# A layer's modulation vector summed by TensorE instead of VectorE, ScalarE and GpSimd

## The chip, the cores and the metric

The kernel runs on one core of one Trainium2 chip. The metric is the device time of one execution in microseconds; lower is better.

## The reference, cut to what matters

Two blocks run over a sequence of 256 tokens of width 1024. The first block has two layers, and each layer scales, shifts and gates by a vector `mod` of six parts that depends on the conditioning `c` alone:

```python
c_act = jax.nn.silu(c)                                  # (1, 1024)
for l in range(2):
    mod = c_act @ w_mod[l] + b_mod[l]                   # w_mod[l]: 1024 x 6144
    shift1, scale1, gate1, shift2, scale2, gate2 = jnp.split(mod[:, None, :], 6, axis=-1)
    h = rms_norm(x, norm1) * (1.0 + scale1) + shift1
    proj = h @ w_in[l]                                  # q, k, u, v and gates
    mix = concat(pool_mixer(u), nsa_mixer(q, kv, gates)) @ w_out[l]
    x = x + gate1 * mix
    h2 = rms_norm(x, norm2) * (1.0 + scale2) + shift2
    x = x + gate2 * (jnp.square(jax.nn.relu(h2 @ w_ff1[l])) @ w_ff2[l])
```

Then a second block follows (a state space branch, an attention branch and a feed forward). The change touches the modulation of the first layer only: parts 0 to 4 of `mod` (shift1, scale1, gate1, shift2, scale2).

## The kernel before, in words

**Products.** Weights come from HBM in pages of 128 partitions by 1024 f32 (512 KB) into the tile `wst`, which has five buffers. ScalarE rounds a page to `wh` (L140), VectorE takes the rest as `wl` (L141), and each product of the model is three TensorE matmuls in a one-pass format (fp32r): high by low, low by high, high by high. All page loads go through one queue (SP), in the order of the program; a load waits until the last reader of the buffer five pages back is done.

**The first two parts of the vector** (shift1 and scale1 of layer 0) are needed before anything else. `start()` walks over four blocks `c` of 256 columns of both parts. `first_mod(c)` loads four pages; VectorE multiplies one half of each page by `c_act` of that row and sums it (L612, L615), ScalarE multiplies the other half and GpSimd sums it (L613, L616, L617). What is left is a sum over partitions, done by eight matmuls against a matrix of ones in `first_norm` (`tr<-cst,acc`), which then transposes 256 columns of the normalized input and makes `hh` and `hl`. Between the blocks run the products for q and k with that block (L89, `acc<-wh,hl` and the like).

**The next three parts** (gate1, shift2, scale2: the list `MODS["mix", 0]`) are summed page by page by `mod_part` while q, k, u, v, the attention and the output product run. Of eight pages of a part five are taken by VectorE (L548) and three by ScalarE and GpSimd (L550, L551), into a tile `macc`; a sum over partitions by matmuls with ones follows (`tr<-cst,macc`, `mal`, `mah`). The parts are generators: `W.load`, which fetches a weight page, advances them by `W.rate` steps, 0 at first and `r0b` = 2 from step 14 of the layer on. The other parts (lists `ff` and `mix` of the next layer) use the same function later.

**PSUM.** Four banks `acc`, two `st`, one `tr`, one `pv`. `pv` holds the transposes in `first_norm`, later the attention's sums over values (`attn_c`), later the transposes of `to_fm`.

**Order.** Each engine runs its instructions in a fixed order that a list scheduler wrote ahead of time: program order is the priority, but an instruction that its model holds ready may go ahead of an earlier one that is not.

Of the kernel before, what the change touches and what calls it, by code (L numbers as in the profile page):

```python
# [24 lines left out]
ALPHA = 2.0 ** 0.25  # L25

SZ = 1024
TU = dict(nst=5, tabc=2, nw=9, nt2=22, raw=1, krest=2, qrest=4, pool2=1, c2=3, c3=1, c4=1, ln=3, uv='uv', pre=[1], nv=5, nv1=0, nv0=0, u0=19.5, du=0.7, ub=2, uc=4, c0=32.5, dc=0.1, w0=36, dw=0.5, comp=22, pool=27, dpool=2, cmpa=32, cmpb=34, dcmp=2, e1=1, e0=1, pta=2, ahead=3, modp=3, rf=0.95, r0=0, r0b=2, r1=0.8, r1b=1.2, rs=14, raw_=4, qrest_=6, u0_=19.5, du_=1.0, comp_=22, pool_=26, cmpa_=31, cmpb_=35, nv_=0, nv0_=0, w0_=32, dw_=0.8, order2='v0 qk0 qk1 qk2 v1 B C x0 x1 z0 x2 z1 x3 z2 z3 g2 g3 pa g0 g1 ps', dts=8, dcd=30, par0=10, par1=40, d0=50, dd=2, db=3, dc2=5, ss0=73, ds=4.2, scb=5, sx=3, sr=6, sg=3.5, sy=3.5, sn=8, sf=300, mf0=5, modp1=99, rf1=0.5, pool2_=3, c3_=2, c4_=3, nv1_=2, dpool_=2, dcmp_=1, dc_=0.4, cap=4, ub_=2.5, c0_=32.5, pta_=4)
NST, NW = TU['nst'], TU['nw']
NT2, NT4, NS5 = TU['nt2'], 5, 20  # L30

# [30 lines left out]
def tile_two_blocks(ctx: ExitStack, tc: tile.TileContext, I, out, stop=None, dbg=None):  # L62
# [452 lines left out]
    V.reciprocal(cact, cact)  # L515
    V.tensor_tensor(cact, cact, csrc, op=OP.mult)

    parc = [small.tile([128, NPS], FT, name=f"parc{l}", bufs=1) for l in range(DEPTH)]
    par = {}

# [5 lines left out]
    def PS(l, n):  # L526
        a, w = SC_[n]
        return parc[l][:, a:a + w]
# [9 lines left out]
    def mod_part(l, q, eng):  # L538

        acc = t4([128, D], "macc")  # L540
        G.memset(acc, 0.0)
        if q in (2, 5):
            nc.sync.dma_start(acc[0:1, :], I["b_mod"][l:l + 1, q * D:(q + 1) * D])
        for k in range(8):
            st = wp.tile([128, SZ], FT, name="wst", bufs=NST)
            nc.sync.dma_start(st, I["w_mod"][l, k * 128:(k + 1) * 128, q * D:(q + 1) * D])
            if eng is V or k % eng:
                V.scalar_tensor_tensor(acc, st, cact[:, k:k + 1], acc, op0=OP.mult, op1=OP.add)  # L548
            else:
                A.activation(st, st, AF.Copy, scale=cact[:, k:k + 1])  # L550
                G.tensor_tensor(acc, acc, st, op=OP.add)  # L551
            yield
        if q in (2, 5):
            gt = t4([128, D], "mgate")
            parts = []
            for n in range(2):
                ns = slice(n * 512, (n + 1) * 512)
                ah, al = t2([128, 512], "mah", FR), t2([128, 512], "mal", FR)
                A.activation(ah, acc[:, ns], AF.Copy)
                G.tensor_tensor(al, acc[:, ns], ah, op=OP.subtract)  # L560
                parts.append((ah, al))
            for _ in range(3):
                yield
            for n, (ah, al) in enumerate(parts):
                b = bank("tr")
                mm(b, ones_r, al, True)
                mm(b, ones_r, ah, False, True)
                A.activation(gt[:, n * 512:(n + 1) * 512], b, AF.Copy)
            MC[l, q] = gt
        else:  # L570
            for _ in range(2):
                yield
            b = bank("tr")
            for j in range(8):
                mm(b[:, j * 64:(j + 1) * 64], acc[:, j * 128:(j + 1) * 128], ones[:, 0:64], j == 0, True)
            c = small.tile([128, 8], FT, name="mcol", bufs=6)
            i = {0: 0, 1: 1, 3: 2, 4: 3}[q]
            V.tensor_tensor(c, b.rearrange("p (j n) -> p j n", j=8)[:, :, 0], PS(l, "bmod")[:, i * 8:i * 8 + 8], op=OP.add)
            if q in (1, 4):
                V.scalar_tensor_tensor(c, c, 1.0, PS(l, "norm1" if q == 1 else "norm2"), op0=OP.add, op1=OP.mult)  # L580
            MC[l, q] = c

    ones_r = cp.tile([128, 128], FR, name="ones_r")

# [16 lines left out]
        xn = rms(t)  # L601
        later(TU["ln"], lambda: to_fm(t, xn, hi, lo, MC[l, q0 + 1], MC[l, q0]))

    def first_mod(c):

        acc = [t2([128, 512], "acc0") for _ in range(2)]
        for j in range(4):
            st = wp.tile([128, SZ], FT, name="wst", bufs=NST)
            nc.sync.dma_start(st, I["w_mod0"][c, j])
            sv, k = [st[:, i * 512:(i + 1) * 512] for i in range(2)], 2 * j  # L610
            if j == 0:
                V.tensor_scalar(acc[0], sv[0], cact[:, k:k + 1], None, op0=OP.mult)  # L612
                A.activation(acc[1], sv[1], AF.Copy, scale=cact[:, k + 1:k + 2])  # L613
            else:
                V.scalar_tensor_tensor(acc[0], sv[0], cact[:, k:k + 1], acc[0], op0=OP.mult, op1=OP.add)  # L615
                A.activation(sv[1], sv[1], AF.Copy, scale=cact[:, k + 1:k + 2])  # L616
                G.tensor_tensor(acc[1], acc[1], sv[1], op=OP.add)  # L617
        return acc

    def first_norm(xn, acc, hi, lo, c):  # L620

        b = bank("tr")
        for i in range(2):
            for j in range(4):
                mm(b[:, j * 64:(j + 1) * 64], acc[i][:, j * 128:(j + 1) * 128], ones[:, 0:64], i == 0 and j == 0, i == 1)
        m = small.tile([128, 4], FT, name="mcol0", bufs=2)
        bm = PS(0, "bmod")[:, 0:16].rearrange("p (q k) -> p q k", q=2)
        V.tensor_tensor(m.rearrange("p (q k) -> p q k", q=2), b[:, :256].rearrange("p (q k n) -> p q k n", q=2, k=2)[:, :, :, 0],
                        bm[:, :, 2 * c:2 * c + 2], op=OP.add)
        V.scalar_tensor_tensor(m[:, 2:4], m[:, 2:4], 1.0, PS(0, "norm1")[:, 2 * c:2 * c + 2], op0=OP.add, op1=OP.mult)  # L630
        b = bank("pv")
        for k in range(2):
            f = 256 * c + 128 * k
            for t in range(2):
                T.transpose(b[:, k * 256 + t * 128:k * 256 + t * 128 + 128], xn[t][f // 512][:, f % 512:f % 512 + 128], ident)
        hf = t2([128, 512], "hf")
        for k in range(2):
            ks = slice(k * 256, (k + 1) * 256)
            V.tensor_scalar(hf[:, ks], b[:, ks], m[:, 2 + k:3 + k], m[:, k:k + 1], op0=OP.mult, op1=OP.add)
        split(fl(hi[:, 2 * c:2 * c + 2]), fl(lo[:, 2 * c:2 * c + 2]), hf, A)  # L640

    def hybrid_layer(l, hilo, between, done):
# [273 lines left out]
        def attn_c(t, br, h0, pT):  # L916

            nh = 4 // (t + 1)
            first = (t, br) not in pvs
            if first:  # L920
                pvs[t, br] = bank("pv")
            bo = pvs[t, br]
            for i in range(4):
                kt, h = i % (t + 1), h0 + i // (t + 1)
                mm(bo[:, h * 64:(h + 1) * 64], pT[:, i * 128:(i + 1) * 128], vS[kt][:, 2 * br - 2 + h // 4, :],
                   first and i == 0, kt == t)
            if h0 + nh == 8:
                wg = wgs[t]
                V.reciprocal(wg[:, br], sms[t][:, br])
                V.tensor_tensor(wg[:, br], wg[:, br], gS[t].rearrange("p (h b) -> p h b", b=3)[:, :, br], op=OP.mult)  # L930
                add_out(t, bo.rearrange("p (h d) -> p h d", h=8), br, V if br == 2 else None)
# [93 lines left out]
        def start():  # L1025

            accs = {n: [bank("acc") for _ in range(2)] for n in "qk"}
            acc = first_mod(0)
            first_norm(xn0, acc, hi, lo, 0)
            for c in range(4):  # L1030
                for n in "qk":
                    wh, wl = W.next()
                    if n == "q" and c < 3:
                        acc = first_mod(c + 1)
                    for k in range(2):
                        for t in range(2):
                            ah, al = act(2 * c + k, t)
                            o = accs[n][t]
                            mm(o, al, wh[:, k], c == 0 and k == 0)
                            mm(o, ah, wl[:, k], False)  # L1040
                            mm(o, ah, wh[:, k], False, c == 3 and k == 1)
                        tick()
                        yield
                    if n == "q" and c < 3:
                        first_norm(xn0, acc, hi, lo, c + 1)
                if c == TU["tabc"]:
                    nc.sync.dma_start(cst[:, 256:], I["cst"][:, 256:])
                    load_par(0)
# [65 lines left out]
    for t in range(2):  # L1114
        nc.sync.dma_start(xs[t], I["x"][0, t * 128:(t + 1) * 128, :])
    V.tensor_copy(ones_r, ones)
    nc.sync.dma_start(parc[1], I["parc"][1])
    h0 = new_h()
    xn0 = [rms(t) for t in range(2)]
    W.rate = TU["r0"]  # L1120
    W.extra.extend(mod_part(*m, TU["modp"]) for m in MODS["mix", 0])
    h1, h2_ = [], []

    def between0(c):
# [636 lines left out]
```

## Time and profile before

| | |
|---|---|
| time, median of 3 runs (range) | 1282.55 us (1280.6 to 1288.57) |
| the profiled execution | 1284.53 us |
| its span, first to last instruction | 1282.4 us |
| TensorE busy, mean granted clock | 1179.8 us (92%), 0.967 |
| VectorE / ScalarE / GpSimd busy | 895.9 / 642.4 / 237.0 us |

The span is what the trace covers; 2.1 us of the profiled execution lie outside it. A matmul of 512 columns is shown as about 0.39 us at the full clock and 0.63 us at half of it, with overlapping records; the distance from one start to the next is what it costs. A matmul of f32 operands (not fp32r) shows as two records, each of two passes over its columns.

### The profile page before, as it was taken

The numbers are of one execution on the slowest core, as the hardware profiler recorded it, in microseconds if no ns is written. First come the engines' busy times: TensorE is split into PE (matmuls) and PEld (weight loads), VectorE is DVE, ScalarE is ACT, GpSimd is POOL, SyncE is SP. The second block draws the span as 40 slices with busy tenths as digits, with TensorE's granted clock in tenths as the row PEclk, the third lists the DMA queues.
The fourth block names the chain that finished last, engine by engine and source line by source line (L and its number), as shares of the span: only waits on it lengthen the run. The fifth ranks groups of instructions, "written<-read, shape, count | busy, mean of one in ns | idle before, by whom it ended". The sixth has DMA issues, their size and how long they took to land.

```text
span 1282.4 us, 19159 instructions
## 1 busy us (share of the span) xinstructions
PE 1179.8 (92%) x7188; PEld 1037.6 (81%) x7188; DVE 895.9 (70%) x1446; ACT 642.4 (50%) x1070; POOL 237.0 (18%) x233
## 2 busy tenths in 40 slices
PE   4878898999898899999999999988898899999997
PEld 3656776899787788789998999977688888799896
DVE  5777798887758768764545738799999557754544
ACT  4346355444535554744543545485675434544440
POOL 3553322112315101210100000011112001210101
PEclk9788889999999999999999999989899899999999
DMA  7855667889878534566663663564466753666640
GB/s 268 284 174 180 230 214 230 292 297 330 289 218 266 189 99 119 190 207 192 181 193 101 216 200 102 195 174 139 135 191 189 258 151 98 226 210 188 183 145 33
DMA packets 101780, 249.18 MB, mean 194 GB/s; under 512 B 9780, under 2 KB 15028, under 8 KB 101688
## 3 DMA queue, kind: packets, MB, share of 16 engines
q1 hardware_dynamic: 100904, 247.12, 60.6%
q8 instruction: 56, 0.92, 0.3%
q10 hardware_dynamic: 784, 0.85, 0.2%
q14 instruction: 36, 0.29, 0.1%
HBM read 246.03 MB, written 1.11 MB: 193 GB/s over the span
## 4 chain that ended last, share of the span: by engine, by line
PE 38%; issue 10%; DVE 8%; ACT 1%; POOL 1%; DMA 0%; DVEq 0%; POOLq 0%; ACTq 0%
PE acc L89 23%; PE st L89 12%; DVE wl L141 2%; DVE R L1444 1%; DVE cv L1330 1%; PE pv L89 1%; DVE G L1433 1%; DVE R L1446 1%; ACT wh L140 1%; POOL yss L119 0%; DVE ytmp L1465 0%; DMA wst<-in_w_up_dram 0%; PE tr L89 0%; POOL fr L380 0%; DVE yg L1477 0%
## 5 line engine op out<-in xcount | busy, mean ns | idle before, releaser
L141 DVE TENSOR_TENSOR wl<-wst,wh 128x1024 fp32r<-128x1024 f32 (+3 forms) x340 | 418.6, 1244 | 164.7 <-ACT wh L140 163.7
L140 ACT ACTIVATE wh<-wst 128x1024 fp32r<-128x1024 f32 (+3 forms) x340 | 352.1, 1048 | 314.2 <-PE acc L89 98.1
L89 PE MATMUL st<-hh,wh 128*128 128x256 f32 x576 | 163.0, 283 | 0.0
L89 PE MATMUL st<-hl,wh 128*128 128x256 f32 x576 | 163.0, 283 | 0.0
L89 PE MATMUL st<-hh,wl 128*128 128x256 f32 x576 | 163.0, 283 | 0.0
L89 PE MATMUL acc<-wh,frl 128*128 128x512 f32 x384 | 151.8, 395 | 2.4 <-DVE frl L381 2.3
L89 PE MATMUL acc<-wl,frh 128*128 128x512 f32 x384 | 150.6, 392 | 0.0
L89 PE MATMUL acc<-wh,frh 128*128 128x512 f32 x384 | 150.3, 391 | 0.0
L380 POOL TENSOR_TENSOR fr<-fr 128x512 f32<-128x512 f32 x48 | 64.7, 1349 | 384.7 <-ACT frh L379 376.4
L89 PE MATMUL acc<-hh,wl 128*128 128x256 f32 x416 | 122.1, 294 | 1.4 <-DVE wl L141 1.4
L89 PE MATMUL acc<-hl,wh 128*128 128x256 f32 x416 | 119.0, 286 | 0.0
L89 PE MATMUL acc<-hh,wh 128*128 128x256 f32 x416 | 118.7, 285 | 0.0
L89 PEld LDWEIGHTS st<-hh,wl 128*128 128x128 f32 x576 | 110.5, 192 | 0.7
L89 PEld LDWEIGHTS st<-hl,wh 128*128 128x128 f32 x576 | 110.5, 192 | 0.7
L89 PEld LDWEIGHTS st<-hh,wh 128*128 128x128 f32 x576 | 110.5, 192 | 0.0
L89 PE MATMUL acc<-wl,hh 128*128 128x512 f32 (+3 forms) x224 | 90.6, 405 | 13.1 <-DVE wl L141 13.1
L89 PE MATMUL acc<-wh,hl 128*128 128x512 f32 (+3 forms) x224 | 90.2, 413 | 12.4 <-ACT wh L140 9.9
L548 DVE SCALAR_TENSOR_TENSOR macc<-wst,cact,macc 128x1024 f32<-128x1024 f32 x70 | 91.7, 1311 | 7.5 <-DMA wst<-in_w_mod_dram 3.9
L89 PE MATMUL acc<-wh,hh 128*128 128x512 f32 (+3 forms) x224 | 90.6, 405 | 0.0
L89 PEld LDWEIGHTS acc<-wh,frl 128*128 128x128 f32 x384 | 72.6, 189 | 19.6 <-DVE frl L381 5.4
L89 PEld LDWEIGHTS acc<-wh,frh 128*128 128x128 f32 x384 | 72.5, 189 | 15.5
L89 PEld LDWEIGHTS acc<-wl,frh 128*128 128x128 f32 x384 | 72.5, 189 | 14.0
(328 smaller groups left out, 2289.6 us busy)
## 6 DMA issues: line engine op xcount, KB each, us to landing
wst<-in_w_ff_dram SPq DMA_DIRECT2D x128, 512.0 KB, 4.4
wst<-in_w_mod_dram SPq DMA_DIRECT2D x96, 512.0 KB, 4.6
wst<-in_w_in_dram SPq DMA_DIRECT2D x92, 512.0 KB, 4.8
wst<-in_w_up_dram SPq DMA_DIRECT2D x32, 512.0 KB, 4.3
wst<-in_w_down_dram SPq DMA_DIRECT2D x32, 512.0 KB, 4.3
wst<-in_w_out_dram SPq DMA_DIRECT2D x24, 512.0 KB, 4.2
R<-rows SPq DMA_DIRECT2D x32, 256.0 KB, 5.4
wst<-in_w_proj_ssd_dram SPq DMA_DIRECT2D x16, 512.0 KB, 4.7
```

The source lines that it names most:

```text
L89: T.matmul(o, l, r, start=start, stop=stop, skip_group_check=True)
L140: A.activation(h[:, :kc * n], st[:, :kc * n], AF.Copy)
L141: V.tensor_tensor(l[:, :kc * n], st[:, :kc * n], h[:, :kc * n], op=OP.subtract)
L380: G.tensor_tensor(r, r, r, op=OP.mult)
L548: V.scalar_tensor_tensor(acc, st, cact[:, k:k + 1], acc, op0=OP.mult, op1=OP.add)
L1330: V.scalar_tensor_tensor(v[:, a:e], u[:, a + j - 2:e + j - 2], w[:, j:j + 1], v[:, a:e], op0=OP.mult, op1=OP.add)
L1433: V.scalar_tensor_tensor(gm[:, i], cl, dt_[:, t, 32 + a0 + i:33 + a0 + i], gm[:, i], op0=OP.mult, op1=OP.add)
L1444: V.scalar_tensor_tensor(E[:, i], E[:, i], sums[:, t, h:h + 1], u[:, i], op0=OP.subtract, op1=OP.min)
L1446: V.tensor_tensor(E, E, ssd.pop(("G", g, t, sub)), op=OP.mult)
```

## The change

The five parts of layer 0's vector that are used up to its feed forward are summed by TensorE in f32. `c_act` is spread once over 32 columns for each of its eight blocks (`cb`), so a matmul of `cb[:, k]` (128 by 32) with a weight page gives 32 equal rows of the partial sum, in one quarter of a PSUM bank's partitions.

`first_rows(c)` replaces `first_mod(c)`: the two halves of each of four pages go to quarters 0 and 1, or 2 and 3, of bank `st`, 512 columns each. A copy by ScalarE and four matmuls with a matrix that picks one row of each quarter (`sel`) then give the columns. The first two blocks' rows are requested before the first `first_norm`, later ones after the k product of each block.

`mod_sums` replaces `mod_part` for the three parts of `MODS["mix", 0]`: each page is one step, of four matmuls of 256 columns, the four quarters of its columns side by side in the four quarters of bank `pv`. Two pages are requested ahead. For a gate, the bias row is added by a DMA into the copied rows and four matmuls with `sel_q`; for a column part, eight matmuls of two columns. The rate from step 14 on is 3 steps a page, not 2, and `attn_c` first lets a part that holds `pv` finish (`while summing: W.step()`). The parts of the lists `ff` and `("mix", 1)` stay with `mod_part`.

```diff
-r0b=2
+r0b=3
+    cb = cp.tile([128, 8, 32], FT, name="cb")
+    V.tensor_copy(cb, cact[:, :, None].to_broadcast([128, 8, 32]))
+    sel = cp.tile([128, 2], FT, name="sel")
+    sel_q = cp.tile([128, 4, 128], FT, name="sel_q")
...
+    def mod_sums(l, q):
+        def load(k):
+            st = wp.tile([128, SZ], FT, name="wst", bufs=NST)
+            nc.sync.dma_start(st, I["w_mod"][l, k * 128:(k + 1) * 128, q * D:(q + 1) * D])
+            return st
+        summing.add((l, q))
+        ts = deque(load(k) for k in range(2))
+        b = bank("pv")
+        for k in range(8):
+            yield
+            st = ts.popleft()
+            for j in range(4):
+                mm(b[j * 32:(j + 1) * 32, :256], cb[:, k], st[:, j * 256:(j + 1) * 256], k == 0, k == 7)
+            if k + 2 < 8:
+                ts.append(load(k + 2))
+        acc = t2([128, 256], "mrow")
+        A.activation(acc, b[:, :256], AF.Copy)
+        summing.discard((l, q))
+        if q in (2, 5):
+            nc.scalar.dma_start(acc[1:128:32, :], I["b_mod"][l, q * D:(q + 1) * D].rearrange("(j n) -> j n", j=4))
+            gt = t4([128, D], "mgate")
+            yield
+            for n in range(2):
+                b = bank("tr")
+                for j in range(2):
+                    mm(b[:, j * 256:(j + 1) * 256], sel_q[:, 2 * n + j], acc, j == 0, True)
+                A.activation(gt[:, n * 512:(n + 1) * 512], b, AF.Copy)
+            MC[l, q] = gt
+        else:
+            yield
+            b = bank("tr")
+            for j in range(8):
+                mm(b[:, 2 * j:2 * j + 2], acc[:, (j % 2) * 128:(j % 2) * 128 + 128], ident[:, 32 * (j // 2):32 * (j // 2) + 2], j == 0, True)
+            mod_columns(l, q, b[:, :16].rearrange("p (j n) -> p j n", j=8)[:, :, 0])
...
-    def first_mod(c):
-        acc = [t2([128, 512], "acc0") for _ in range(2)]
+    def first_rows(c):
+        b = bank("st")
         for j in range(4):
             st = wp.tile([128, SZ], FT, name="wst", bufs=NST)
             nc.sync.dma_start(st, I["w_mod0"][c, j])
-            sv, k = [st[:, i * 512:(i + 1) * 512] for i in range(2)], 2 * j
-            if j == 0:
-                V.tensor_scalar(acc[0], sv[0], cact[:, k:k + 1], None, op0=OP.mult)
-                A.activation(acc[1], sv[1], AF.Copy, scale=cact[:, k + 1:k + 2])
-            else:
-                V.scalar_tensor_tensor(acc[0], sv[0], cact[:, k:k + 1], acc[0], op0=OP.mult, op1=OP.add)
-                A.activation(sv[1], sv[1], AF.Copy, scale=cact[:, k + 1:k + 2])
-                G.tensor_tensor(acc[1], acc[1], sv[1], op=OP.add)
-        return acc
+            for i in range(2):
+                k = 2 * j + i
+                r = slice((k % 4) * 32, (k % 4) * 32 + 32)
+                mm(b[r], cb[:, k], st[:, i * 512:(i + 1) * 512], k < 4, k >= 4)
+        rows = t2([128, 512], "rows0")
+        A.activation(rows, b, AF.Copy)
+        return rows
...
         b = bank("tr")
-        for i in range(2):
-            for j in range(4):
-                mm(b[:, j * 64:(j + 1) * 64], acc[i][:, j * 128:(j + 1) * 128], ones[:, 0:64], i == 0 and j == 0, i == 1)
+        for j in range(4):
+            mm(b[:, 2 * j:2 * j + 2], rows[:, j * 128:(j + 1) * 128], sel, j == 0, True)
...
             if first:
+                while summing:
+                    W.step()
                 pvs[t, br] = bank("pv")
...
-            acc = first_mod(0)
-            first_norm(xn0, acc, hi, lo, 0)
+            rows = [first_rows(0), first_rows(1)]
+            first_norm(xn0, rows[0], hi, lo, 0)
...
-                    if n == "q" and c < 3:
-                        acc = first_mod(c + 1)
...
                     if n == "q" and c < 3:
-                        first_norm(xn0, acc, hi, lo, c + 1)
+                        first_norm(xn0, rows[c + 1], hi, lo, c + 1)
+                    if n == "k" and c < 2:
+                        rows.append(first_rows(c + 2))
...
+    for i in range(2):
+        V.reduce_sum(sel[:, i:i + 1], ident[:, 0:128:32], axis=AX.X)
+    for j in range(4):
+        V.tensor_tensor(sel_q[:, j], ident[:, 32 * j:32 * j + 1].to_broadcast([128, 128]),
+                        ident[:, 32 * j + 1:32 * j + 2].to_broadcast([128, 128]), op=OP.add)
...
-    W.extra.extend(mod_part(*m, TU["modp"]) for m in MODS["mix", 0])
+    W.extra.extend(mod_sums(*m) for m in MODS["mix", 0])
```

## Rows read from the trace of the kernel before

**Rows 1.** The page's busy time by engine: busy us, share of the span, instructions.

```profile
PE 1179.8 (92%) x7188; PEld 1037.6 (81%) x7188; DVE 895.9 (70%) x1446; ACT 642.4 (50%) x1070; POOL 237.0 (18%) x233
```

**Rows 2.** Busy time by stretch: stretch, length, engines, granted clock, DMA share, GB/s.

```profile
0.00:22.50 22.50, 6.14 (x24) 4.88 (x24) 10.21 (x21) 9.81 (x18) 7.90 (x14) 1.00 0.75 266
22.50:70.70 48.20, 41.47 (x168) 32.58 (x168) 34.31 (x41) 23.17 (x34) 27.71 (x45) 0.86 0.84 287
70.70:137.10 66.40, 47.09 (x256) 37.56 (x254) 51.64 (x122) 31.65 (x68) 24.45 (x21) 0.87 0.54 172
137.10:190.00 52.90, 49.71 (x286) 42.54 (x287) 45.46 (x105) 23.27 (x60) 14.52 (x7) 0.89 0.67 217
220.00:1282.40 1062.40, 1009.01 (x6339) 899.35 (x6337) 729.37 (x1128) 536.53 (x865) 157.28 (x144) 0.98 0.60 188
```

**Rows 3.** Waits of PE from 0 to 190: total us, times, longest.

```profile
PE acc L89 <- DVE wl L141: 11.0, 5, 5.4
PE pv L635 <- DVE xn L596: 10.7, 2, 10.4
PE tr L89 <- DVE acc L615: 6.0, 3, 3.5
PE tr L89 <- DVE chv L837: 4.5, 1, 4.5
```

**Rows 4.** Costliest groups by line, 0 to 70.7: busy us, mean ns, idle before.

```profile
L617 POOL TENSOR_TENSOR acc<-acc,wst 128x512 f32<-128x512 f32 x12 | 19.1, 1595 | 24.1 <-ACT wst L616 17.6 <-ACT acc L613 6.0
...
L615 DVE SCALAR_TENSOR_TENSOR acc<-wst,cact,acc 128x512 f32<-128x512 f32 x12 | 16.2, 1350 | 0.4
...
L89 PE MATMUL tr<-cst,acc 128*128 128x64 f32 x64 | 10.6, 337 | 6.0 <-DVE acc L615 6.0
```

**Rows 5.** The tile macc, 0 to 190: ns min/median/max, first and last start.

```profile
L89 PE MATMUL tr<-cst,macc x32: 217/275/323, 165.7 to 181.5; 128*128 128x64 f32 x32
L548 DVE SCALAR_TENSOR_TENSOR macc<-wst,cact,macc x17: 1234/1280/1286, 86.8 to 185.5; 128x1024 f32<-128x1024 f32 x17
L551 POOL TENSOR_TENSOR macc<-macc,wst x9: 2353/2380/3261, 82.8 to 170.8; 128x1024 f32<-128x1024 f32 x9
```

**Rows 6.** Timeline of PE near 76 and 160: start us, us, operation.

```profile
76.30 0.80 PE L89 MATMUL acc<-wl,hh 128*128 128x512 f32 x1 [5.43 <-DVE wl L141]
...
159.15 1.02 PE L89 MATMUL tr<-vbd,pcT 128*128 128x512 f32 x2
159.60 0.79 PE L89 MATMUL acc<-wl,mh 128*128 128x512 f32 x1
160.23 0.39 PE L89 MATMUL acc<-wh,mh 128*128 128x512 f32 x1
160.46 0.40 PE L89 MATMUL acc<-wh,ml 128*128 128x512 f32 x1
```

**Rows 7.** Timeline of PE near 747, where outputs are quarters of a bank.

```profile
746.47 0.28 PE L89 MATMUL acc<-hl,wh 128*128 128x256 f32 x1
746.59 0.28 PE L89 MATMUL acc<-hh,wh 128*128 128x256 f32 x1
746.79 0.63 PE L89 MATMUL st<-cst,av 128*32 128x128 f32 x8
747.36 1.08 PE L89 MATMUL tr<-av,cst 128*128 128x32 f32 x8
```

**Rows 8.** Timeline of DVE near 82.

```profile
80.76 0.28 DVE L682 TENSOR_TENSOR sq<-sq,hr 128x128 f32<-128x128 f32 x1
...
82.89 2.47 DVE L682 TENSOR_TENSOR sq<-sq,hr 128x128 f32<-128x128 f32 x1 [0.90 <-POOL hr L119]
```

**Rows 9.** Timeline of POOL at the same time.

```profile
82.83 2.38 POOL L551 TENSOR_TENSOR macc<-macc,wst 128x1024 f32<-128x1024 f32 x1
```

**Rows 10.** Busy time in two stretches of one granted clock each; columns as in group 2.

```profile
40.80:51.00 10.20, 9.58 (x31) 7.38 (x29) 7.72 (x10) 3.75 (x6) 3.10 (x3) 0.50 0.70 210
51.00:57.80 6.80, 4.82 (x29) 3.78 (x27) 4.54 (x8) 2.10 (x3) 2.42 (x2) 1.00 1.00 369
```

More of the change, by code (lines that the diff above doesn't have):

```diff
@@ L27 @@
 SZ = 1024
-TU = dict(nst=5, tabc=2, nw=9, nt2=22, raw=1, krest=2, qrest=4, pool2=1, c2=3, c3=1, c4=1, ln=3, uv='uv', pre=[1], nv=5, nv1=0, nv0=0, u0=19.5, du=0.7, ub=2, uc=4, c0=32.5, dc=0.1, w0=36, dw=0.5, comp=22, pool=27, dpool=2, cmpa=32, cmpb=34, dcmp=2, e1=1, e0=1, pta=2, ahead=3, modp=3, rf=0.95, r0=0, r0b=2, r1=0.8, r1b=1.2, rs=14, raw_=4, qrest_=6, u0_=19.5, du_=1.0, comp_=22, pool_=26, cmpa_=31, cmpb_=35, nv_=0, nv0_=0, w0_=32, dw_=0.8, order2='v0 qk0 qk1 qk2 v1 B C x0 x1 z0 x2 z1 x3 z2 z3 g2 g3 pa g0 g1 ps', dts=8, dcd=30, par0=10, par1=40, d0=50, dd=2, db=3, dc2=5, ss0=73, ds=4.2, scb=5, sx=3, sr=6, sg=3.5, sy=3.5, sn=8, sf=300, mf0=5, modp1=99, rf1=0.5, pool2_=3, c3_=2, c4_=3, nv1_=2, dpool_=2, dcmp_=1, dc_=0.4, cap=4, ub_=2.5, c0_=32.5, pta_=4)
+TU = dict(nst=5, tabc=2, nw=9, nt2=22, raw=1, krest=2, qrest=4, pool2=1, c2=3, c3=1, c4=1, ln=3, uv='uv', pre=[1], nv=5, nv1=0, nv0=0, u0=19.5, du=0.7, ub=2, uc=4, c0=32.5, dc=0.1, w0=36, dw=0.5, comp=22, pool=27, dpool=2, cmpa=32, cmpb=34, dcmp=2, e1=1, e0=1, pta=2, ahead=3, modp=3, rf=0.95, r0=0, r0b=3, r1=0.8, r1b=1.2, rs=14, raw_=4, qrest_=6, u0_=19.5, du_=1.0, comp_=22, pool_=26, cmpa_=31, cmpb_=35, nv_=0, nv0_=0, w0_=32, dw_=0.8, order2='v0 qk0 qk1 qk2 v1 B C x0 x1 z0 x2 z1 x3 z2 z3 g2 g3 pa g0 g1 ps', dts=8, dcd=30, par0=10, par1=40, d0=50, dd=2, db=3, dc2=5, ss0=73, ds=4.2, scb=5, sx=3, sr=6, sg=3.5, sy=3.5, sn=8, sf=300, mf0=5, modp1=99, rf1=0.5, pool2_=3, c3_=2, c4_=3, nv1_=2, dpool_=2, dcmp_=1, dc_=0.4, cap=4, ub_=2.5, c0_=32.5, pta_=4)
 NST, NW = TU['nst'], TU['nw']
@@ L575, in mod_part @@
                 mm(b[:, j * 64:(j + 1) * 64], acc[:, j * 128:(j + 1) * 128], ones[:, 0:64], j == 0, True)
[L576 to L581, printed above, removed]
+            mod_columns(l, q, b.rearrange("p (j n) -> p j n", j=8)[:, :, 0])
@@ new lines, in tile_two_blocks @@
+    summing = set()
+    def mod_sums(l, q):
[32 more added lines that the diff above has]
+            mod_columns(l, q, b[:, :16].rearrange("p (j n) -> p j n", j=8)[:, :, 0])
@@ L583, in tile_two_blocks, with mod_columns @@
+    def mod_columns(l, q, src):
+        c = small.tile([128, 8], FT, name="mcol", bufs=6)
+        i = {0: 0, 1: 1, 3: 2, 4: 3}[q]
+        V.tensor_tensor(c, src, PS(l, "bmod")[:, i * 8:i * 8 + 8], op=OP.add)
+        if q in (1, 4):
+            V.scalar_tensor_tensor(c, c, 1.0, PS(l, "norm1" if q == 1 else "norm2"), op0=OP.add, op1=OP.mult)
+        MC[l, q] = c
     ones_r = cp.tile([128, 128], FR, name="ones_r")
@@ L609, in first_mod, with first_norm @@
             nc.sync.dma_start(st, I["w_mod0"][c, j])
-            sv, k = [st[:, i * 512:(i + 1) * 512] for i in range(2)], 2 * j
-            if j == 0:
-                V.tensor_scalar(acc[0], sv[0], cact[:, k:k + 1], None, op0=OP.mult)
-                A.activation(acc[1], sv[1], AF.Copy, scale=cact[:, k + 1:k + 2])
-            else:
-                V.scalar_tensor_tensor(acc[0], sv[0], cact[:, k:k + 1], acc[0], op0=OP.mult, op1=OP.add)
-                A.activation(sv[1], sv[1], AF.Copy, scale=cact[:, k + 1:k + 2])
-                G.tensor_tensor(acc[1], acc[1], sv[1], op=OP.add)
-        return acc
-    def first_norm(xn, acc, hi, lo, c):
-        b = bank("tr")
-        for i in range(2):
-            for j in range(4):
-                mm(b[:, j * 64:(j + 1) * 64], acc[i][:, j * 128:(j + 1) * 128], ones[:, 0:64], i == 0 and j == 0, i == 1)
[L626 to L631, printed above, removed]
+            for i in range(2):
[5 more added lines that the diff above has]
+        return rows
+    def first_norm(xn, rows, hi, lo, c):
+        b = bank("tr")
+        for j in range(4):
+            mm(b[:, 2 * j:2 * j + 2], rows[:, j * 128:(j + 1) * 128], sel, j == 0, True)
+        bt = bank("pv")
         for k in range(2):
@@ L634, in first_norm @@
             for t in range(2):
-                T.transpose(b[:, k * 256 + t * 128:k * 256 + t * 128 + 128], xn[t][f // 512][:, f % 512:f % 512 + 128], ident)
+                T.transpose(bt[:, k * 256 + t * 128:k * 256 + t * 128 + 128], xn[t][f // 512][:, f % 512:f % 512 + 128], ident)
+        m = small.tile([128, 4], FT, name="mcol0", bufs=2)
+        bm = PS(0, "bmod")[:, 0:16].rearrange("p (q k) -> p q k", q=2)
+        V.tensor_tensor(m.rearrange("p (q k) -> p q k", q=2), b[:, :8].rearrange("p (q k n) -> p q k n", q=2, k=2)[:, :, :, 0],
+                        bm[:, :, 2 * c:2 * c + 2], op=OP.add)
+        V.scalar_tensor_tensor(m[:, 2:4], m[:, 2:4], 1.0, PS(0, "norm1")[:, 2 * c:2 * c + 2], op0=OP.add, op1=OP.mult)
         hf = t2([128, 512], "hf")
@@ L638, in first_norm @@
             ks = slice(k * 256, (k + 1) * 256)
-            V.tensor_scalar(hf[:, ks], b[:, ks], m[:, 2 + k:3 + k], m[:, k:k + 1], op0=OP.mult, op1=OP.add)
+            V.tensor_scalar(hf[:, ks], bt[:, ks], m[:, 2 + k:3 + k], m[:, k:k + 1], op0=OP.mult, op1=OP.add)
         split(fl(hi[:, 2 * c:2 * c + 2]), fl(lo[:, 2 * c:2 * c + 2]), hf, A)
```

## The prediction

> **What bounds the kernel now.** I read the page's busy time first [rows 1]: TensorE (PE) is busy for 1179.8 of 1282.4 us, so over the whole run only work or waits of PE count. The change touches layer 0 up to its feed forward, so I cut the span there [rows 2]. From 220 us on PE stands idle 53 of 1062 us and the code is the same before and after; I let that part stand. The first 190 us hold 45.6 us of idle PE: 16.4 in stretch A (0 to 22.5, the first product of q starts at its end), 6.7 in B (to 70.7, the products of q and k), 19.3 in C (to 137.1, u, v and most of the attention, up to the first output product) and 3.2 in D (to 190). Read the DVE column beside it: in C VectorE is busy for 51.6 of 66.4 us, the stage in which it is nearest to full. The waits say the same [rows 3]: nearly all idle time of PE ends on VectorE: the low halves of weights (11.0 us), the first partial sums of `first_mod` (6.0), a copy in the compression (4.5). The 10.4 us for the first `xn` are the load of x, and stay. So now VectorE's queue bounds A to C, and PE bounds D and what follows. The granted clock is 0.86, 0.87 and 0.89 in B, C and D [rows 2]; between the two levels that is 13.5, 17.3 and 11.6 us at 1.2 GHz (twice what is missing from 1, times the length).
>
> **The change part by part.** *Taken from VectorE and GpSimd.* In A and B 12 sums of 1.35 us on VectorE and 12 of 1.6 on GpSimd [rows 4]; in C and D 15 of 1.28 on VectorE (the 17 of the row less two of the next list) and 9 of 2.38 on GpSimd [rows 5]. A GpSimd sum costs VectorE more than its place: the same 128x128 operation takes 0.28 us, and 2.47 us when it starts 0.06 us after a GpSimd sum [rows 8, 9]. So VectorE gets some 19 us of 51.6 + 45.5 back in C and D, and the stretching besides.
>
> *Put on TensorE: the price of one matmul.* An f32 matmul with 512 columns is two records. With an fp32r matmul between, they fill 159.15 to 160.23; less the 0.23 of that one (160.23 to 160.46) they cost 0.85 us [rows 6], that is 0.107 for each 128 columns of a record. Alone, the 96 matmuls of 256 columns of the three parts would cost 96 x 0.43 = 41 us and the 32 of 512 columns of the first blocks 27 us. Do quarters run beside each other? Eight records of 128 columns that go to two quarters start at 746.79, and the next thing at 747.36 [rows 7]: 0.57 us, where one after another they would need 0.86. Two quarters thus do run together: 4 x 0.107 = 0.43 plus 0.14 to change over, where the step into them is 0.20 against the usual 0.12. For four quarters no row exists: the bounds are 41 us (no overlap), 20 (as the row, two) and 10.2 (four). I take four, since nothing in the row tells the second quarter from a third. With 0.14 to 0.18 for the change of mode at each of 24 pages, 4 us, the three parts cost 14.5 us.
>
> The page "TensorEngine Tiling (Array Packing)" of the Trainium skill, section "Tiling Modes", says that a change of mode drains TensorE, which speaks against bursts of four small matmuls between full ones; the 0.14 us of the row are in agreement. "TensorE: Matmul & The Clock Gate", Part 3, gives 2.38 times for three column tiles, not 3; scaled so, four would give 3.2, and the estimate for the three parts would be 2.7 us higher. No run here shows either.
>
> *Stretch A* (22.5 us): no VectorE sums in front of the first column sums, which are half as many (4 matmuls in place of 8). But eight pages, not four, are read before the first `first_norm` if the scheduler leaves PE in program order. At 1.42 us a page (524288 bytes at the 369 GB/s of the stretch with the DMA engines full [rows 10]) the second four cost 5.7 us, less the some 3 us that the chain is shorter. If it takes the first block ahead of them, A is 3 us shorter. I take 0, bounds -3 and +4. The new VectorE work (`cb`, `sel`, `sel_q`: seven small operations, under 2 us) lies where VectorE is busy 10.2 of 22.5 us; 1 us if it stands ahead of `xn`, within the bounds.
>
> *Stretch B* (48.2 us): PE loses most of its idle time, 5.7 of 6.7, since blocks 2 and 3 are summed ahead, on PE, with no VectorE chain of four sums left. It gets two blocks of first rows: 13.7 us alone, 6.8 in pairs as the halves of one page, 3.4 if two landed pages go side by side; I take 5, plus 1.1 for changes of mode. Column sums fall from 64 records in 10.6 us [rows 4] to 32; three of four blocks are in B, so 4.0 less. Of 13.5 us at the lower clock, 10.2 lie between 40.8 and 51.0 [rows 10] and follow waits for partial sums; with PE fed I give back half of them, 3.4 us of time. Sum: -5.7 + 5 + 1.1 - 4.0 - 3.4 = -7.0. Bounds: all matmuls alone and no clock back +6, everything well -13.
>
> *Stretch C* (66.4 us): the waits for low halves (11.0 us in all, the longest, 5.4, before the first product of u at 76.3 [rows 3, 6]) and for the copy (4.5) shrink, as VectorE has 9 sums less here and no stretching. I take away 12 of 19.3 us; the rest is chains of the attention, of which the free-standing mod matmuls can fill some 3. PE gets the 14.5 us, and 0.8 for the gate's f32 broadcast (4 x 0.43, for 4 x 0.23). The columns cost the same: 32 records before [rows 5], 32 after. Half of the 17.3 us at the lower clock back, at PE's share of 0.7, is 3 to 4. Sum: -12 - 3 + 15.3 - 4 = -3.7. The price if that cover is gone: all 15.3 us stand on the path. Bounds: -16 and +12.
>
> *Stretch D* (52.9 us): PE is full; what goes is the last column sum. The 32 records begin at 165.7 and end after 181.5 [rows 5]; the second 16 stand behind the last output product, and its result keeps bank `tr`, so the next transposes wait 0.9 us more. With the higher rate the 28 steps (9 a part and one) are spent within ten weight pages of step 14, so shift2 and scale2 are there long before. I take -3, bounds 0 and -5.
>
> *Queues.* SP issues the same 24 pages of the three parts, three a weight page and not two; four pages a chunk of u or v are 5.7 us of transfer. What frees their buffers is PE, not VectorE or GpSimd. New waits: a mod matmul waits on PE for its page, and behind it stand the products of u and v and the attention's; `attn_c` waits for `pv`. In C the DMA engines are at 0.54 [rows 2], so there is room; cost 0, up to 6 us (below). The bias row goes from SP to ScalarE's queue, after the copy; the gate is used only in D, so 0, at most its issue.
>
> **Sum.** 0 - 7.0 - 3.7 - 3 = -13.7 us. The profiled execution took 1284.5, so 1270.8; it lies 2.0 over the median of the three runs, so 1269 us there. A measurement of this kernel tells no change from one of about 1%, 12.8 us.
>
> **The rivals.** *1. The pages bound u and v.* Seven chunks at 5.7 us are 40 us; they start at 76.3 now [rows 6], so C has 61 us for them and for the attention behind them. With that part at its present pace C gains nothing and loses up to 3, and all in all -7 to -10: about 1275. For it: PE waits for pages at its own queue's head, with only five buffers. Against: DMA at 0.54 in C, and a list scheduler that can put other ready work first.
>
> *2. The clock and the idle time come back in full.* If PE is dense from the first page on, B is 13 us shorter and C 8 to 10, with D 3 to 5: some -26, 1257. For it: every lower stretch lies behind a wait on VectorE. Against: the compression and attention chains in C stay.
>
> *3. The quarters don't run together, and TensorE becomes the bound.* Alone, the three parts cost 41 + 4, not 14.5, and the first blocks 27, not 10: +47 on the same -13.7 gives +33, 1316. It decides at two quarters: there, +10 and +4 eat the gain exactly. Against: the pairs of [rows 7]. For: no row has four, and all four read 128 partitions at once.
>
> *4. Nothing comes of it.* PE's added 24 us (10 + 1 to 2 + 14.5 + 0.8 less 5.3 column sums, with changes of mode) just fill the 24 us of idle time that is not the first load or attention, without clock gains: -2 to +3, 1282. The clock of C would show 0.87 again.
>
> **How the numbers follow.** The forecast (1262 to 1274) 0.48, the pages 0.16, the full gain 0.14, nothing 0.14, quarters apart 0.08 (half of it between two and no overlap, 1283 to 1316). The range leaves out the last and the best corner of the second: 1252 to 1284. Faster by over 1% (under 1269.7): 0.36 of the forecast's, all of the second: 0.50. Slower by over 1% (over 1295): 0.06. Within: 0.44.
>
> **What would show it.** Right: four mod matmuls' first records starting within some 0.03 us and the next four 0.21 later; end of the k products near 63 us (now 70.7); no DVE operation of 0.28 us at over 2 us in C; idle PE in C near 5 us; no column sum of `tr` behind the last output product. Wrong: `wst` DMAs as what ends PE's waits in C (rival 1), starts of the quarters 0.1 or 0.2 us apart (rival 3), a shifted span after 220 us (the scheduler wrote another order there, which I put at zero).

## The result, and the profile after

The change made the kernel slower by 1.1%: 1296.93 us (median of 4 runs) against 1281.57 of the kernel before, run beside it (4 runs too), a ratio of 1.0112 [1.0066, 1.0158]. 1269 had been forecast, and 1284 was the top of the range. The profiled execution took 1298.61 us, 14.1 more than the one before; its span is 1296.8 us.

The page's busy time after, to be read beside [rows 1]:

```profile
PE 1205.4 (93%) x7416; PEld 1040.5 (80%) x7416; DVE 856.1 (66%) x1422; ACT 624.2 (48%) x1050; POOL 186.3 (14%) x207
```

VectorE and GpSimd lost what the change takes from them (895.9 to 856.1 and 237.0 to 186.3 us), and TensorE got 25.6 us; 24 had been forecast. The stretches of [rows 2], after, with the granted clock and the DMA share behind the five engines:

```profile
0.00:22.50 22.50, 11.68 (x56) 4.22 (x56) 5.64 (x24) 6.82 (x14) 2.18 (x10) 1.00 0.85 297
22.50:70.70 48.20, 39.13 (x164) 26.26 (x165) 24.22 (x41) 18.85 (x28) 16.10 (x37) 0.88 0.78 272
70.70:137.10 66.40, 63.42 (x448) 43.36 (x451) 31.77 (x110) 22.91 (x59) 7.15 (x10) 0.96 0.66 211
137.10:190.00 52.90, 47.80 (x305) 39.30 (x296) 40.31 (x95) 21.82 (x57) 4.12 (x3) 0.94 0.62 204
190.00:220.00 30.00, 17.71 (x70) 13.73 (x70) 26.18 (x27) 7.33 (x15) 6.16 (x6) 0.72 0.66 220
220.00:1282.40 1062.40, 1018.74 (x6356) 908.17 (x6355) 721.64 (x1119) 546.48 (x880) 149.60 (x140) 0.98 0.59 185
```

The third line looks like a success: in stretch C the idle time of PE fell from 19.3 to 3.0 us and the clock rose from 0.87 to 0.96. The fifth holds the failure. It is the start of layer 0's feed forward, which I had shown no row of. The same line of the kernel before, and then what SP and VectorE do there:

```profile
190.00:220.00 30.00, 26.40 (x121) 20.70 (x120) 24.92 (x32) 17.97 (x32) 5.18 (x3) 0.98 0.72 235
```

PE is idle for 12.3 of the 30 us instead of 3.6, so 8.7 us more, and the granted clock is 0.72, not 0.98. The two overlap and can't be added: the clock stands at 0.51 from 202.5 to 220, and for 8.9 of these 17.5 us PE does nothing. It works for 8.6 us there, so the lower level costs at most some 4 us (an estimate: half of that time). SP's queue after (start, time from the first to the last of the group, operation, count):

```profile
166.40 42.03 SPq L551 DMA_DIRECT2D wst<-in_w_mod_dram  x16
209.42 0.38 SPq L135 DMA_DIRECT2D wst<-in_w_ff_dram  x1
210.74 0.33 SPq L551 DMA_DIRECT2D wst<-in_w_mod_dram  x1
212.39 0.38 SPq L135 DMA_DIRECT2D wst<-in_w_ff_dram  x1
```

For 42 us SP asks for sixteen pages of the modulation vector and for no page of feed-forward weights. In the kernel before the two mostly alternate from 182.00 on:

```profile
182.00 0.38 SPq L135 DMA_DIRECT2D wst<-in_w_ff_dram  x1
183.87 0.33 SPq L546 DMA_DIRECT2D wst<-in_w_mod_dram  x1
186.82 0.38 SPq L135 DMA_DIRECT2D wst<-in_w_ff_dram  x1
188.05 0.72 SPq L546 DMA_DIRECT2D wst<-in_w_mod_dram  x1
```

VectorE after, at the same place, and PE's longest wait from 190 to 240 (total, times, longest):

```profile
196.93 4.68 DVE L644 TENSOR_SCALAR xn<-x,ss 128x512 f32<-128x512 f32 x2 [0.67 <-POOL ss L119]
201.52 9.19 DVE L553 SCALAR_TENSOR_TENSOR macc<-wst,cact,macc 128x1024 f32<-128x1024 f32 x7
...
216.77 1.23 DVE L141 TENSOR_TENSOR wl<-wst,wh 128x1024 fp32r<-128x1024 f32 x1 [0.22 <-ACT wh L140]
```
```profile
PE tr L89 <- DVE macc L553: 8.5, 1, 8.5
```

Seven sums of 1.3 us in a row, of parts that are needed only later, stand in VectorE's queue ahead of the low halves for the feed forward. PE's longest wait is for such a part too: the sum of `macc` over partitions stands ahead of the next feed-forward products in PE's own order.

**Where the time went.** I mark five places in PE's order: the first product of q, the first transposes of the k products (`kd`), the first feed-forward product, the first product of its second half (`frl`), and the first product of q in layer 1. Before, they lie at 22.5, 70.5, 194.1, 223.3 and 397.5 us, after at 23.6, 62.5, 192.6, 239.0 and 408.1. Stretch A is 1.1 longer and B 9.1 shorter, C with D takes 130.1 in place of 123.7, and the start of the feed forward 46.5 in place of 29.2. Up to its first product the changed kernel is 1.6 us ahead; the next 29 cost it 17.3. The rest of that feed forward gives 5.1 back, presumably as its sums are already made (not tried), and from layer 1 on the changed kernel is 3.8 longer, which no run explains.

### The profile page after: what moved, and what is told of

It reads as the page before. It is cut to its first block, busy times and chain, and to the rows that moved or that the text cites. A ratio compares the mean times of both kernels' runs of the same rounds, so it can differ in the third digit from the quotient of the medians.

```text
span 1296.8 us, 19495 instructions
## 1 busy us (share of the span) xinstructions
PE 1205.4 (93%) x7416; PEld 1040.5 (80%) x7416; DVE 856.1 (66%) x1422; ACT 624.2 (48%) x1050; POOL 186.3 (14%) x207
## 4 chain that ended last, share of the span: by engine, by line
PE 37%; issue 10%; DVE 8%; ACT 1%; POOL 1%; DMA 1%; DVEq 0%; POOLq 0%; ACTq 0%; SPq 0%
PE acc L89 23%; PE st L89 12%; DVE wl L141 2%; DVE R L1497 1%; DVE cv L1383 1%; PE pv L89 1%; DVE R L1499 1%; DVE G L1486 1%; ACT wh L140 1%; POOL yss L119 0%; DMA wst<-in_w_up_dram 0%; DVE ytmp L1518 0%; DMA R<-rows 0%; PE tr L89 0%; POOL fr L380 0%
## 5 line engine op out<-in xcount | busy, mean ns | idle before, releaser
L89 PEld LDWEIGHTS acc<-wh,frl 128*128 128x128 f32 x384 | 72.6, 189 | 19.3 <-DVE frl L381 5.1
L89 PEld LDWEIGHTS acc<-wh,frh 128*128 128x128 f32 x384 | 72.4, 189 | 15.3
L89 PEld LDWEIGHTS acc<-hh,wl 128*128 128x128 f32 x416 | 81.2, 195 | 3.7 <-DVE wl L141 1.8
L89 PEld LDWEIGHTS acc<-wl,frh 128*128 128x128 f32 x384 | 72.6, 189 | 14.1
```

The lines of the kernel that those rows point to most:

```text
L89: T.matmul(o, l, r, start=start, stop=stop, skip_group_check=True)
```

## The experiments

The cause that the program suggests is a counter in the function that loads a weight page:

```python
self.due += self.rate
while self.due >= 1.0 and self.extra:
    self.due -= 1.0
    self.step()
```

`extra` is the list of parts still to be summed. When it is empty, `due` goes on growing. The parts of the `ff` list are added late; by then the counter stands at 4 in the kernel before and at 23 in the changed one, counted from the two programs: 15 weight pages at rate 2 give 30, of which 26 steps were taken; 15 at rate 3 give 45, of which 22 were taken. (In either program six more steps are called for directly and don't lower the counter.) The first feed-forward page then sets off 23 steps at once. All ratios below are to the kernel before, on the same chip. Experiments 1 and 2 shared one chip; 3, 4 and 5 each had another, so between those only ratios are compared.

**1. The counter alone, both ways.** `e1_due4` is the changed kernel, `e2_before_due23` the kernel before; both set the counter where the list is added:

```diff
+        if l == 0:
+            W.due = 4.0     # 23.0 in e2
         W.extra.extend(mod_part(*m, V) for m in MODS["ff", l])
```

> The changed kernel, with the step counter set to 4.0 (its value in the kernel before) at the moment the feed forward's list of parts is appended, instead of the 23.0 that piles up while the list is empty. Theory A (the backlog puts 18 modulation pages ahead of the second feed forward weight page): the first down product comes 15 to 19 us earlier than in the changed kernel (239.0 us), and the time falls to 1276 to 1283. Theory B (the 15 us of added TensorE work surface there, whatever the page order): within 4 us of the changed kernel, 1293 to 1299.

> The kernel before, with nothing changed but the step counter set to 23.0 at that moment (4.0 of its own). Theory A: the same run of pages stands ahead of the feed forward's weights, so 10 to 18 us slower than before, 1292 to 1300, without any of the change's matmuls. Theory B: within 4 us of before.

Measured: 1280.91 us, 0.9976 [0.9955, 0.9997], and 1300.84 us, 1.0131 [1.0103, 1.016]. Setting one number removes the loss, and puts it into a kernel that has nothing else of the change. The lines of 190 to 220 us, of `e1_due4` and of `e2_before_due23`:

```profile
190.00:220.00 30.00, 27.70 (x131) 22.21 (x129) 22.51 (x30) 20.23 (x34) 6.38 (x6) 1.00 0.66 211
```
```profile
190.00:220.00 30.00, 13.26 (x54) 10.12 (x52) 23.18 (x24) 4.74 (x9) 6.70 (x6) 0.65 0.72 247
```

So 1.0112 less 0.9976, some 17 us, is the backlog. Without it the change is worth 3 us, not 14.

**2. Each half alone.** `e3_rows_only` keeps `first_rows`, and has `mod_part` and the rate of 2 for the later parts; `e4_sums_only` keeps `mod_sums` and the rate of 3, with `first_mod` as before and the counter at 4.

```diff
# e3
-    W.extra.extend(mod_sums(*m) for m in MODS["mix", 0])
+    W.extra.extend(mod_part(*m, TU["modp"]) for m in MODS["mix", 0])
-r0b=3
+r0b=2
```

> The first two parts by TensorE (first_rows), the three later parts as before (mod_part, rate 2). Theory A: the q and k products end some 8 us earlier, as in the changed kernel (62.5 against 70.5), and this stays to the end: 1271 to 1276. Theory B (what is won early is lost later in any case): 1279 to 1285.

> The three later parts by TensorE at rate 3 with the counter set to 4.0, the first two parts as before (first_mod). Theory A: the stretch from the end of the k products to the first feed forward product gets 6 us longer as in the changed kernel, nothing else: 1284 to 1291. My prediction's own sum for these stretches was 6.7 shorter: 1273 to 1277.

Measured: 1275.65 us, 0.9946 [0.9921, 0.9972], and 1289.65 us, 1.0044 [1.0019, 1.0068]. The first rows on TensorE are a gain of 7 us. The later sums with their rate of 3 are a loss of 6, where my sum had made them a gain.

**3. Is it the bursts, the rate, the leftover steps, or the first block's place?** `f1_quarter_work` is `e1_due4` with matmuls in two of eight pages of each part (the other six are loaded and left out of the sum, so the vector is incomplete); `f2_rate2` is `e1_due4` at rate 2; `f3_rows_no_due` is `e3_rows_only` with the counter kept at nought while the list is empty; `f4_norm_first` is `f3_rows_no_due` with the second block's rows behind the first `first_norm`.

```diff
# f1
-            for j in range(4):
+            for j in range(4 if k in (0, 7) else 0):
# f2
-r0b=3
+r0b=2
# f3 (and g1, g2, g4, h1)
             self.due += self.rate
             while self.due >= 1.0 and self.extra:
                 self.due -= 1.0
                 self.step()
+            if not self.extra:
+                self.due = 0.0
# f4
-            rows = [first_rows(0), first_rows(1)]
+            rows = [first_rows(0)]
             first_norm(xn0, rows[0], hi, lo, 0)
+            rows.append(first_rows(1))
```

> The kernel with the counter at 4.0 (e1_due4), with the matmuls of 18 of the 24 modulation pages left out (pages 1 to 6 of each part are loaded and not summed, so the vector is incomplete). A burst of four holds TensorE for 0.57 us, so 18 are 10.3 us. Theory C (TensorE is full between the k products and the feed forward, the bursts stand on the path): 8 to 12 us less than e1_due4, 1269 to 1273. Theory D (they fill waiting time, and what keeps the gain away is the chains of the attention and of the norm at the end): within 3 us of e1_due4, 1278 to 1284.

> e1_due4 with the rate at 2 steps a page and not 3, nothing else. Theory C: the same work at another place, within 3 us of e1_due4 (1278 to 1284). The rival of the prediction that the transfers bound u and v at rate 3: 4 to 8 us less than e1_due4, 1273 to 1277.

> First two parts by TensorE, later ones as before at rate 2 (e3_rows_only), and the counter is set to zero whenever the list is empty, in both layers (4.0 and 25.2 at the two feed forwards before). Theory A says that any stored steps push pages ahead of the feed forward's: the 4 steps of layer 0 are some 3 pages, the 11 of layer 1 one whole part. 2 to 8 us less than e3_rows_only: 1268 to 1274. If the pages there fit into waiting time of the queue: as e3_rows_only, 1274 to 1278.

> f3_rows_no_due with the first first_norm ahead of the second block's rows, not behind them. If the second block's four pages of matmuls hold the first product back (it starts at 23.6 to 25.8 in the kernels with first_rows, at 22.5 before): first product at 20 to 22, 2 to 4 us less than f3_rows_no_due. If the page transfers or the lower clock set the start: within 1 us of it.

Measured: `f1_quarter_work` 1277.75 us, 0.9965 [0.9945, 0.9986]; `f2_rate2` 1281.27, 0.9971 [0.9948, 0.9995]; `f3_rows_no_due` 1275.27, 0.9941 [0.9918, 0.9964]; `f4_norm_first` 1278.41, 0.9960 [0.9933, 0.9987]. Leaving out 18 of 24 bursts, 10.3 us at 0.57, gave back about 1.4 (0.0011, inside the intervals). From the first transposes of the k products to the first feed-forward product, the traces of `e1_due4` and of `f1_quarter_work` show:

```profile
64.10:192.60 128.50, 115.98 (x765) 86.14 (x766) 80.61 (x220) 52.45 (x129) 13.57 (x15) 0.95 0.62 203
```
```profile
63.70:189.50 125.80, 109.34 (x621) 87.32 (x621) 81.22 (x221) 51.75 (x129) 13.34 (x15) 0.91 0.62 211
```

The stretch is 2.7 us shorter; PE works 6.6 us less, stands idle 3.9 us more, and has a lower clock. So PE's time in the bursts is mostly not what sets the end at rate 3. The few leftover steps show no price, and neither does the place of the second block (the first product of q came at 24.9 us, not sooner). The lower rate showed nothing in the time.

**4. The counter kept down, at both rates.** `g1_rate2_no_fill` and `g4_rate3_no_fill` are the changed kernel at rate 2 and 3, `g2_before_no_fill` is the kernel before, all three with the edit of f3.

> The changed kernel at rate 2, with the counter set to nought whenever no step is listed, so that it can't run up. Backlog theory: the changed kernel's loss (ratio 1.011) is gone and the time is that of the changed kernel with the counter set to 4: 0.995 to 0.999 of the kernel before (1277 to 1283 us). Rival, that the later parts' bursts of TensorE cost what they take: 1.003 or more. It isn't expected to reach the run with the row alone (0.994).

> The kernel before, with the counter set to nought whenever no step is listed: it stood at 4 when the feed-forward list came. Backlog theory with a price per step: 19 steps more cost 17 us, so 4 fewer give at most 3.6 us: ratio 0.997 to 1.001. Rival, that any early step delays the first feed-forward pages and the kernel before has the same loss in small: 0.990 to 0.996, and then the row-alone runs got their gain from elsewhere than thought.

> The changed kernel at its own rate of 3, with the counter set to nought whenever no step is listed (also in the second layer, where it stood at 44). Backlog theory: as with the counter set to 4 in the first layer alone, 0.995 to 0.999 (1277 to 1283 us); the second layer's list has 11 steps, so its part is under 2 us either way. Rival, that the second layer's backlog costs as the first one's did: 0.985 to 0.993.

Measured: 1273.69 us, 0.9926 [0.9897, 0.9956]; 1282.35, 1.0005 [0.9981, 1.0029]; 1281.09, 0.9982 [0.9956, 1.0007]. The kernel before had no such loss, and layer 1's larger counter cost nothing that the intervals would show. The first came out better than I expected, the best time of the study, though not apart from the row alone (0.9941). Here the rate did show, by 0.0056 between `g1_rate2_no_fill` and `g4_rate3_no_fill`; in experiment 3 it had not (0.9971 and 0.9976).

The stretch from `kd` to the first feed-forward product, parted at the first output product, shows what the sums do there. In order, with the columns of [rows 2]: the kernel before, the changed one, `g1_rate2_no_fill`.

```profile
70.50:137.10 66.60, 47.29 (x257) 37.68 (x255) 51.64 (x122) 31.85 (x69) 24.65 (x21) 0.87 0.54 172
137.10:194.10 57.00, 53.81 (x302) 45.84 (x303) 47.95 (x109) 26.49 (x65) 14.52 (x7) 0.89 0.65 211
```
```profile
62.50:145.80 83.30, 75.55 (x537) 52.82 (x538) 42.56 (x140) 32.24 (x75) 9.53 (x12) 0.94 0.65 212
145.80:192.60 46.80, 41.70 (x230) 34.57 (x229) 38.26 (x81) 18.12 (x53) 4.12 (x3) 0.93 0.56 179
```
```profile
64.90:130.80 65.90, 60.94 (x416) 42.73 (x416) 37.57 (x117) 27.79 (x69) 8.34 (x12) 0.97 0.63 197
130.80:185.80 55.00, 54.74 (x352) 42.66 (x351) 34.20 (x97) 23.23 (x59) 3.12 (x3) 0.94 0.51 171
```

Length less PE's busy time is its idle time. At rate 2 PE works 115.7 us of 120.9 where it worked 101.1 of 123.6: 14.6 us more work, 17.3 less idle time, 2.7 saved, which is within what two profiled executions differ by (the kernel before with `g2_before_no_fill`'s edit took 120.1). At rate 3 it works 117.3 us, hardly more, but 12.9 are idle. Its waits up to the feed forward, after:

```profile
PE acc L89 <- DVE wl L141: 7.2, 3, 4.8
PE pv L460 <- DVE xn L644: 5.1, 1, 5.1
PE tr L89 <- DMA mrow<-in_b_mod_dram: 2.3, 1, 2.3
```

The second and the third are new. At rate 2 PE's waits for `xn` and the bias row come to 0.3 us and nothing. The two rates also differ in where the bursts lie: at rate 3 the last one starts at 140.7 us, ahead of the first output product (145.8), at rate 2 they last to 159.8 (the first output product is at 130.8). But that the bursts, had they been left beside the output product, would have covered the wait is not shown: `g4_rate3_no_fill` has its last burst at 140.0 and no wait for `xn`, only one of 3.7 us for `ml`, the low half of the attention's result, and the run of experiment 5 waits 5.0 us there without any burst.

**5. The rate without the new sums.** `h1_rows_rate3` is `f3_rows_no_due` with `r0b=3`.

> The row alone, with the old sums on VectorE and GpSimd, the counter kept at nought while nothing is listed, and the rate raised from 2 to 3. In the profiled runs so far the stretch from the first transposes of the k products to the first feed-forward product took 128.2 to 130.2 us in the four kernels with all of the new sums at rate 3 and 120.1 to 123.7 in those at rate 2, old sums or new. Theory of the transfers: a third page of the modulation behind each page of weights holds up the weights of u, v and the output; then the stretch is 126 to 130 us here too, and the time 0.997 to 1.002 of the kernel before. Rival, that TensorE's bursts at rate 3 make it, by standing between the attention's products: the stretch stays at 120 to 124 and the time at 0.992 to 0.996, as with the row alone.

Measured: 1291.02 us, 1.0085 [1.0055, 1.0114]. Its rows, under those of `f3_rows_no_due`:

```profile
63.30:131.60 68.30, 49.74 (x269) 39.85 (x268) 53.16 (x123) 33.42 (x71) 24.41 (x21) 0.86 0.53 175
131.60:185.40 53.80, 50.56 (x302) 42.82 (x303) 48.23 (x108) 28.13 (x67) 13.61 (x7) 0.95 0.68 216
```
```profile
63.00:139.70 76.70, 54.70 (x268) 43.67 (x268) 57.59 (x127) 37.31 (x75) 33.36 (x24) 0.84 0.64 208
139.70:198.00 58.30, 52.16 (x303) 44.65 (x304) 46.16 (x109) 24.43 (x63) 6.51 (x4) 0.91 0.52 165
```

The old sums at rate 3 make the stretch 12.9 us longer (135.0 against 122.1): 6.3 of idle PE and 6.6 of busy PE for the same records (571 and 571), at a lower clock. So the third page behind each weight page has a price without any burst of TensorE, and the rival falls; the price is above what the theory of the transfers gave (126 to 130 us, 0.997 to 1.002). Whether it is the transfers, or the sums that VectorE and GpSimd make the earlier for them, is not shown. PE's waits in the two, `f3_rows_no_due` first, go to VectorE's results, and none ends on a weight page:

```profile
PE acc L89 <- DVE wl L141: 7.5, 3, 4.7
PE acc L89 <- DVE ml L106: 4.3, 2, 2.9
```
```profile
PE acc L89 <- DVE wl L141: 9.4, 4, 4.7
PE acc L89 <- DVE ml L106: 7.4, 3, 5.0
```

The run also turns my reading of the new sums round: at rate 3 they are 0.0103 better than the old ones (0.9982 and 1.0085, 13 us), at rate 2 they are level with them (0.9926 or 0.9971, and 0.9941).

## Why the prediction was wrong

**The step that failed** is the one on stretch D and the queues: "With the higher rate the 28 steps are spent within ten weight pages of step 14, so shift2 and scale2 are there long before", with "cost 0" for SP, and everything after 220 us left out because "the code is the same before and after". The first half came true (the last burst is at 140.7 us). I didn't ask what the counter does once the steps are spent: it runs to 23, and puts sixteen pages or more that nobody yet waits for ahead of the feed forward's. The code there is the same, but its state is not. That is 17 us (experiment 1). My list of what would be wrong had "a shifted span after 220 us", with the scheduler as its cause; it had no rival with a price for it.

**A second term put at nothing was the rate itself**, in the passage on the queues: "In C the DMA engines are at 0.54 [rows 2], so there is room; cost 0, up to 6 us (below)". The stretch from `kd` to the first feed-forward product takes 121.0 and 122.5 us in the two traces with the new sums at rate 2 (`g1_rate2_no_fill`, `f2_rate2`), and 128.2 to 130.2 in the four at rate 3; with the old sums it is 120.1 to 123.7 at rate 2 and 135.0 at rate 3. So rate 3 costs the stretch some 7 us with the new sums and 13 with the old. Rival 1 (the pages) had about this price, but its sign did not show: no wait of PE in C or D ends on a weight page.

**Stretches C and D** were mis-sized by 13 us: 130.1 - 123.7 = +6.4, where I had -6.7. The mechanism was there: C's idle time between 70.7 and 137.1 fell by 16.3 us (forecast 15), the clock of C and D rose to 0.96 and 0.94, no column sum stands behind the last output product (in the kernel before none did either: the second 16 start at 179.9 and end by 181.8 us, ahead of the last output products, so that reading of [rows 5] was wrong). Two terms were off. PE's work in the two rose by 16.1, not by 11.3 (15.3 less 4 for the clock): from start to start the bursts fill 16.0 us, not 14.5, as many are split by other work; the gate's broadcast takes 2.0, where the old one took 1.65, so 0.4 more and not 0.8; and twelve more products of `hh` (2.9 at 0.24) stand behind the mark than before. The sum of these is 3.2 above the 16.1, where 4 had been taken off for the clock. And the idle time fell by 9.6 us where I had taken off 18, D's 3 included, since D got a new wait of 5.1 us and C one of 2.3, of which the traces at rate 2 show 0.3 and nothing. At rate 2 the idle time fell by 17.3 and PE's work rose by 14.6: in the time my rival 4, "nothing comes of it", held for the sums, though the clock of C rose, which it had denied. That the bursts are what took the 17.3 us there was not tried by leaving them out; at rate 3 leaving out 18 of 24 shortened the stretch by 2.7. The 24 us of added work in that rival are 22 by their own terms.

**Stretch B** gained 9.1 us (forecast 7.0, the k transposes at 62.5 us where I said near 63), of which the twelve products that moved behind the mark are about 3. **Stretch A** lost 1.1 (forecast 0, bounds -3 and +4); `f4_norm_first` shows that the second block's place isn't it. With the row alone at 0.9941 to 0.9946, these two hold.

**The price of a burst** was right. PE after, and the tile:

```profile
74.48 0.64 PE L89 MATMUL pv<-wst,cb 128*32 128x256 f32 x8
75.05 0.50 PE L89 MATMUL acc<-wl,hh 128*128 128x512 f32 x1
```
```profile
L89 PE MATMUL pv<-wst,cb x192: 378/379/502, 74.5 to 140.7; 128*32 128x256 f32 x192
```

The first records of the four quarters start within 0.02 us of each other, the second ones 0.24 later, and the next product 0.57 after the first. Of rival 3 (quarters apart) nothing is left. One by one the four would take 1.71 us (8 records of 256 columns at 0.107 for 128), so a whole burst runs at 3.0 times that pace. The Trainium skill's 2.38 times for three column tiles ("TensorE: Matmul & The Clock Gate", Part 3), which I had scaled to an estimate of 3.2 for four, lies near it.

**VectorE's stretching** went as forecast: the 128x128 operations of L728 take 272 to 293 ns after, where one had 2.47 us [rows 8]. The waits for low halves shrank from 11.0 to 7.2 us only; the one of 4.8 stands behind VectorE's own wait for a small power by GpSimd (2.02 us there, 1.54 of it idle time of VectorE).

**What stays open.** Whether rate 2 with the new sums is better than rate 3 in the time (one pair says 7 us, the other none), and whether it beats the first rows alone. The traces have the stretch up to the feed forward 6.1 and 7.2 us shorter at rate 2; but behind the first product of `frl` the fourteen traces differ by up to 14.5 us (1055.0 to 1069.5), where little or nothing was changed, and that can hide it. Why rate 3 makes the stretch longer, and the clock in `h1_rows_rate3` lower, is open too.

## What to carry to other kernels

Where background work is paced by a counter, follow the counter through the stretch in which it has nothing to spend, and into the next list: a change that ends the work earlier, or raises its rate, becomes a burst at the next start. Read a change's price past the last place that its code touches, up to where every queue and counter that it feeds is again as it was before. Idle time of the bounding engine is not a gain by itself: here 14.6 us of work from other engines went into 17.3 us of it, and the stretch was shorter by 2.7. Leave the work out once, to see what it costs, before the idle time is counted as room. And price the pace of background pages by a run that changes the pace alone.

## What had not been expected

Four column quarters of TensorE run in step: four f32 matmuls of 256 columns cost 0.57 us with both changes of mode. A stretch can look healed and still be longer: C showed 3.0 us of idle time and a clock of 0.96, while C and D together took 6.4 us more. And the pace of background pages has a price of its own: with the old sums, a third page behind each weight page instead of a second made the stretch to the feed forward 12.9 us longer.
